# Storing six rows of one image over four DMA engines instead of sixteen, in a convolution kernel

## The chip, the cores and the metric

The kernel runs on one core of a Trainium2 chip. The metric is the device time of one execution in microseconds (us). All comparisons are between runs made on the same chip in the same rounds.

The core has 16 DMA engines, which carry everything between memory and the core's buffers. TensorE does the matmuls (PE, its weight loads PEld), VectorE is DVE, ScalarE ACT, GpSimd POOL, and SP issues transfers.

## The reference

A 3x3 convolution with padding 1. There are 16 images of 64 channels, 64 x 64 points each, and 128 output channels, all in float32:

```python
x = randn(16, 64, 64, 64);  weight = randn(128, 64, 3, 3) * 0.1
output[b, co] += weight[co, ci, kh, kw] * x_pad[b, ci, kh:kh+64, kw:kw+64]   # summed over ci, kh, kw
```

The output is 33.5 MB and the input 16.8 MB, so the DMA engines have some 50 MB to carry.

## The kernel before

Images are worked on in eight pairs. A pair's input lies on 128 partitions (2 images x 64 channels), and its output on 128 partitions too (the 128 output channels), with both images side by side in a tile of 2 x 64 x 64 numbers per partition. All transfers are issued by SP. The loads of the first seven pairs are issued at the start; from then on a pair's store is issued when its last DVE addition is done.

```python
for p in range(NP):                       # 8 pairs
    for blk in range(4):                  # 8 row pairs each
        U  = group([(G1, None)])          # matmuls
        ... us = ACT copies of U ...
        A  = group([(G21, 1), (G0, -1)])
        for b2 in range(2):
            nc.vector.tensor_add(ots[p][:, b2, j0:j0+RB, 0, :], A[b2], us[b2])
        Bt = group([(G01, 0), (G2, 2)])
        for b2 in range(2):
            nc.vector.tensor_add(ots[p][:, b2, j0:j0+RB, 1, :], Bt[b2], us[b2])
        parts = {3: (0, 64)} if p < NP - 1 else {1: (0, 32), 3: (32, 64)}
        if blk in parts:                  # the last pair is stored in two halves
            lo, hi = parts[blk]
            keep(nc.sync.dma_start(out_pairs[p, :, :, lo:hi, :], ...[:, :, lo:hi, :]))
            if p == 2: load(LATE)
# ... = cut
```

## Time and profile before

| | before |
|---|---|
| median of the runs | 127.7 us |
| span of the profiled execution | 126.6 us |
| PE busy | 84% |
| last DVE addition ends | 112.8 us |
| last store issued / landed | 112.84 / 125.6 us |
| main DMA queue | 50.63 MB, 95.1% of 16 engines' span |

### The profile page before, as it was taken

How to read it: one execution, taken by the hardware profiler on the slowest of the kernel's cores; microseconds unless marked ns; L12 is line 12 of the kernel's file. 1: busy time of each engine (PE TensorE's matmuls, PEld its weight loads, DVE VectorE, ACT ScalarE, POOL GpSimd, SP SyncE). 2: the span in 40 equal slices, each digit the busy share in tenths (PEclk: the TensorE clock that was granted, in tenths of full speed). 3: DMA queues.
4: the chain of work that ended last, by engine and by line, in shares of the span. 5: the costliest groups of instructions: out<-in, count | busy, mean ns of one | idle time of the engine just before them, and what ended most of it. 6: DMA issues, size and time to landing. Idle time of an engine off the chain costs nothing.

```text
span 126.6 us, 2424 instructions
## 1 busy us (share of the span) xinstructions
PE 106.0 (84%) x978; PEld 55.8 (44%) x978; DVE 84.3 (67%) x135; ACT 65.5 (52%) x98; POOL 33.3 (26%) x22
## 2 busy tenths in 40 slices
PE   0489999999999999999999999999999999920000
PEld 0334555555555555555555555555555555500000
DVE  0287777777777777777877787778777877760000
ACT  4283999998789876666333333336666333300000
POOL 2000395930780075007600660068000000000000
PEclk9999999999999999999999999999999999999555
DMA  4999999999999999999999999999999999999940
GB/s 116 322 422 435 424 430 419 450 419 424 430 440 437 409 442 409 435 435 419 440 414 435 424 419 435 430 435 430 414 430 445 424 424 419 432 417 424 432 184 13
DMA packets 4186, 50.77 MB, mean 401 GB/s; under 512 B 336, under 2 KB 336, under 8 KB 976
## 3 DMA queue, kind: packets, MB, share of 16 engines
q1 hardware_dynamic: 4176, 50.63, 95.1%
q8 instruction: 7, 0.11, 0.3%
q14 instruction: 3, 0.02, 0.0%
HBM read 17.07 MB, written 33.55 MB: 400 GB/s over the span
## 4 chain that ended last, share of the span: by engine, by line
PE 82%; DMA 4%; DVE 2%; issue 1%; DVEq 0%; SPq 0%
PE acc L174 82%; DMA xf<-in_x_dram 4%; DVE ot L194 1%; DVE ss L98 1%; DVEq L230 0%; DVE ot L197 0%; SPq L48 0%; DVEq L194 0%
## 5 line engine op out<-in xcount | busy, mean ns | idle before, releaser
L174 PE MATMUL acc<-xs,Wt 64*128 64x504 f16 (+3 forms) x768 | 88.9, 378 | 0.0
L174 PEld LDWEIGHTS <-Wt 64*128 64x128 f16 x960 | 54.7, 95 | 50.9 <-issue 3.3
L194 DVE TENSOR_TENSOR ot<-acc,ut 128x512 f32<-128x512 f32 x64 | 41.2, 686 | 21.9 <-PE acc L174 18.2
L188 ACT COPY ut<-acc 128x512 f32<-128x512 f32 x64 | 34.4, 590 | 39.7 <-issue 35.2
L197 DVE TENSOR_TENSOR ot<-acc,ut 128x512 f32<-128x512 f32 x64 | 41.1, 683 | 0.2 <-PE acc L174 0.2
L75 ACT CAST xs<-xf 128x1024 f16<-128x1024 f32 (+2 forms) x30 | 30.9, 1065 | 0.7 <-DMA xf<-in_x_dram 0.7
L174 PE MATMUL acc<-ss,Wt 64*128 64x504 f16 (+1 forms) x192 | 27.1, 384 | 1.2 <-DVE ss L98 1.2
L98 POOL TENSOR_TENSOR ss<-xs 128x1024 f16<-128x1024 f16 x8 | 16.8, 2124 | 30.8 <-PE acc L174 30.8
L98 POOL TENSOR_TENSOR ss<-xf 128x1024 f16<-128x1024 f32 x6 | 14.1, 2363 | 23.5 <-DMA xf<-in_x_dram 14.9
L116 PE MATMUL wp<-ident,w 128*64 128x128 f16 x18 | 1.3, 329 | 4.2 <-DVE w L88 4.2
L98 DVE TENSOR_TENSOR ss<-xf 128x512 f16<-128x512 f32 x4 | 2.8, 689 | 2.8 <-DMA xf<-in_x_dram 2.8
L116 PEld LDWEIGHTS <-w 128*64 128x64 f16 x18 | 1.1, 211 | 4.2 <-DVE w L88 4.2
L88 DVE CAST w<-w_raw 128x576 f16<-128x576 f32 x1 | 0.5, 460 | 3.7 <-DMA w_raw<-in_weight_dram 3.7
L118 ACT CAST Wt<-wp 128x384 f16<-128x384 f32 x1 | 0.5, 479 | 2.9 <-PE wp L116 2.9
L75 POOL CAST xs<-xf 128x896 f16<-128x896 f32 x2 | 1.9, 926 | 0.0
L118 ACT ACT_TABLE_LOAD x1 | 1.3, 1283 | 0.7 <-PEq L219 0.7
L123 ACT CAST Wt<-wp 128x384 f16<-128x384 f32 x1 | 0.5, 479 | 0.5 <-DVE Wt L121 0.5
L120 DVE TENSOR_TENSOR Wt<-wp,Wt 128x384 f16<-128x384 f32 x1 | 0.6, 550 | 0.0
L121 DVE TENSOR_TENSOR Wt<-wp,Wt 128x384 f16<-128x384 f32 x1 | 0.5, 547 | 0.0
L124 ACT CAST Wt<-wp 128x384 f16<-128x384 f32 x1 | 0.5, 485 | 0.0
masks.py:199 POOL TENSOR_SCALAR_AFFINE_SELECT ident<-ident 128x128 f16<-128x128 f16 x1 | 0.3, 295 | 0.1
masks.py:197 POOL MEMSET ident<- 128x128 f16 x1 | 0.2, 205 | 0.3 <-POOLq L219 0.3
(4 smaller groups left out, 0.4 us busy)
## 6 DMA issues: line engine op xcount, KB each, us to landing
out_dram<-ot SPq DMA_DIRECT2D x7, 4096.0 KB, 21.1
xf<-in_x_dram SPq DMA_DIRECT2D x7, 2048.0 KB, 21.2
out_dram<-ot SPq DMA_DIRECT2D x2, 2048.0 KB, 13.6
xf<-in_x_dram SPq DMA_DIRECT2D x2, 512.0 KB, 6.1
xf<-in_x_dram SPq DMA_DIRECT2D x1, 576.0 KB, 4.9
xf<-in_x_dram SPq DMA_DIRECT2D x1, 448.0 KB, 7.2
w_raw<-in_weight_dram SPq DMA_DIRECT2D x1, 288.0 KB, 3.0
```

Of the source, the lines that this page charges most:

```text
L75: keep(copy(xs[p][:, lo:hi, :], xf[p][:, lo:hi, :]))
L88: keep(nc.vector.tensor_copy(w16, w_raw))
L98: eng.tensor_add(ss[p][:, lo : lo + n, :], v[:, lo : lo + n, 0, :], v[:, lo : lo + n, 1, :])
L116: nc.tensor.matmul(wp[q : q + 64, k * CO : k * CO + CO], w16[:, t::9], ident)
L118: keep(nc.scalar.copy(wrow(G1), wps[1]))
L120: keep(nc.vector.tensor_sub(wrow(G21), wps[2], wrow(G1)))
L121: keep(nc.vector.tensor_sub(wrow(G01), wps[0], wrow(G1)))
L123: keep(nc.scalar.copy(wrow(G0), wps[0]))
L174: nc.tensor.matmul(tiles[b2][:, lo - j0 : hi - j0, c_lo:c_hi], Wt[p0 : p0 + 64, wi, kw, :], rhs, start=i == 0, stop=i == n - 1,)
L188: keep(nc.scalar.copy(ut, U[b2]))
L194: nc.vector.tensor_add(ots[p][:, b2, j0 : j0 + RB, 0, :], A[b2], us[b2])
L197: nc.vector.tensor_add(ots[p][:, b2, j0 : j0 + RB, 1, :], Bt[b2], us[b2])
```

## The change

Its intent is to move a little of the DMA work from most of the engines to four of them. Pair 5's store (the sixth pair) is cut in four. Six rows of its second image go by two transfers that cover 124 and 4 partitions, and neither number can be divided evenly over 16 engines.

```diff
-                keep(nc.sync.dma_start(
-                    out_pairs[p, :, :, lo:hi, :],
-                    ots[p].rearrange("p b j i c -> p b (j i) c")[:, :, lo:hi, :],
-                ))
+                src = ots[p].rearrange("p b j i c -> p b (j i) c")
+                dst = out_pairs[p]
+                if p == 5:
+                    keep(nc.sync.dma_start(dst[:, 0, :, :], src[:, 0, :, :]))
+                    keep(nc.sync.dma_start(dst[:, 1, 0:58, :], src[:, 1, 0:58, :]))
+                    for q0, q1 in ((0, 124), (124, 128)):
+                        keep(nc.sync.dma_start(dst[q0:q1, 1, 58:64, :], src[q0:q1, 1, 58:64, :]))
+                else:
+                    keep(nc.sync.dma_start(dst[:, :, lo:hi, :], src[:, :, lo:hi, :]))
```

## The prediction

> **What bounds the kernel now.** I read the page's slices first, then its chain that ended last, then the DMA queue's own waits, and last a table of stretches over the end of the run.
>
> In the slices PE and DMA both look full. They are the rows of busy tenths and of moved data, 40 slices of 3.17 us:
>
> ```profile
> PE   0489999999999999999999999999999999920000
> DMA  4999999999999999999999999999999999999940
> GB/s 116 322 422 435 424 430 419 450 419 424 430 440 437 409 442 409 435 435 419 440 414 435 424 419 435 430 435 430 414 430 445 424 424 419 432 417 424 432 184 13
> ```
>
> PE is empty in the last four to five slices while DMA goes on at full rate for most of them. The chain of waits names PE, but it follows compute instructions only and stops where the last one stops:
>
> ```profile
> PE acc L174 82%; DMA xf<-in_x_dram 4%; DVE ot L194 1%; DVE ss L98 1%; DVEq L230 0%; DVE ot L197 0%; SPq L48 0%; DVEq L194 0%
> ```
>
> In order of time its last piece is the DVE addition at 112.22 us, 0.60 us long, so it ends at 112.8. The span is 126.6. The 13.8 us after it belong to the stores. The queue's own waits say the same; L230 is the end of the program:
>
> ```profile
> SPq L230 <- DMA out_dram<-ot: 12.4, 2, 7.5
> ```
>
> The table of stretches shows how that tail runs out. Its columns are the busy times of PE, PEld, DVE, ACT and POOL, the granted clock, the mean share of the 16 DMA engines that is busy, and GB/s:
>
> ```profile
> 100.00:110.00 10.00, 10.00 (x96) 5.26 (x94) 7.57 (x13) 3.58 (x7) 0.00 (x0) 1.00 1.00 424
> ...
> 118.00:120.00 2.00, 0.00 (x0) 0.00 (x0) 0.00 (x0) 0.00 (x0) 0.00 (x0) 0.50 1.03 438
> 120.00:121.00 1.00, 0.00 (x0) 0.00 (x0) 0.00 (x0) 0.00 (x0) 0.00 (x0) 0.50 0.87 369
> 121.00:122.00 1.00, 0.00 (x0) 0.00 (x0) 0.00 (x0) 0.00 (x0) 0.00 (x0) 0.50 0.54 229
> 122.00:123.00 1.00, 0.00 (x0) 0.00 (x0) 0.00 (x0) 0.00 (x0) 0.00 (x0) 0.50 0.24 98
> 123.00:124.00 1.00, 0.00 (x0) 0.00 (x0) 0.00 (x0) 0.00 (x0) 0.00 (x0) 0.50 0.08 33
> 124.00:125.00 1.00, 0.00 (x0) 0.00 (x0) 0.00 (x0) 0.00 (x0) 0.00 (x0) 0.50 0.06 25
> ```
>
> Until 120 us all 16 engines are busy and the rate stays at 424 to 438 GB/s, so the kernel is bound by what the DMA engines carry: 50.63 MB on this queue, 3.164 MB an engine. Then they drop out one after another. A share of 0.06 is one engine of 16, and 25 GB/s is one engine's rate (424/16 = 26.5). So **the end is set by the one engine that is last**, alone for its last 2 us. A transfer over 16 engines gives each the same bytes, but they don't work at the same pace.
>
> To see why, I took the trace's individual transfer records. They don't name their engine, so I joined them into 16 sequences, each record starting where another ended; this is inference. Five sequences finish at about 120.7 to 120.9, two at 121.3 to 121.4, seven at 122.1 to 122.4, one at 123.13 and one at 125.17. The cluster of seven and some others each met one 16 KB instruction fetch (7 of them, 0.88 to 1.01 us each, each on another engine). The last one has no such fetch: from 41 to 111 us, but for a pause about 70 to 77, its 16 KB packets take some 645 ns where the others take 611. So one engine is slow by itself.
>
> **What the Trainium skill says.** "DMA: Bandwidth & Descriptors", section "Why a DMA increments its semaphore by 16 and not by 1": the engines used are the largest k up to 16 that divides the slowest dimension's size on both sides, and on the hardware queues the lowest-numbered k are used. For 124 and for 4 that gives 4, so engines 0 to 3. This trace has only transfers of 128 partitions, with 16 semaphore increments for each of its 21, which agrees as far as it goes; k = 4 is not shown yet. The same page, section "Latency and other measured facts", says that engines 7 and 15 are usually slower in traces and guesses at a cause tied to software queues. The trace agrees that one engine is slow (645 against 611 ns), on a hardware queue; it doesn't show which. "Runtime: NRT & Kernel Launch", section "Instruction fetch mechanics", says that instructions are refilled in 16 KiB blocks by DMA; the seven 16,384-byte packets of the instruction queue agree.
>
> **The change part by part.** Pair 5's 4 MB store, issued at 87.23 us, becomes four: image 0 whole, 58 rows of image 1, and the last six rows of image 1 in two pieces of 124 and 4 partitions. The bytes are the same.
>
> *Issue.* Three more issues on SP at 0.37 us (the issue's duration): 1.1 us on a queue that otherwise waits 36.7 us for DVE between 80 us and the end. At 87.2 the engines still hold most of pair 4's store (issued at 74.42, landing between 91.8 and 95.5), so none runs dry. Cost: 0.
>
> *Semaphores.* The landings use 8 semaphores in turn, so a later transfer takes one again. With three more, pair 6 and the two halves of pair 7 take those of transfers landed by 85 us. Cost: 0. No compute instruction waits for pair 5's store, as its slot is not used again. Cost: 0.
>
> *Bytes moved.* Six rows are 6 x 64 x 4 = 1,536 B a partition, 196,608 B in all. Over 16 engines that is 12,288 B each; over four it is 49,152 B. So engines 4 to 15 lose 12,288 B, and 0 to 3 gain 36,864 B.
>
> *Time of it.* From the records, back to back, a 16,384 B packet takes 608 ns, 8,192 B 306, 4,096 B 153, 2,304 B 90. That is nearly straight, 0.037 ns a byte and a few ns fixed. A 14,848 B packet is then about 551 ns and a 1,536 B one about 62 (estimates). Engines 4 to 15: 8 x (551 - 608) = -456 ns, and one more semaphore write of 9 ns: **-0.45 us** (about -0.47 at the slow engine's pace). Engines 0 to 3: the same -0.45, plus 31 + 1 = 32 packets of 62 ns = +1.98, plus two semaphore writes: **+1.55 us**.
>
> *Sum.* If the slow engine is one of 4 to 15, it ends at 125.17 - 0.45 = 124.7. The latest that one of engines 0 to 3 could have ended is 123.13; with 1.55 it comes to 124.7 as well, no later. If they are of the usual 120.7 to 122.4, they come to 122.3 to 124.0. So the end moves by about -0.45 us: 127.7 - 0.45 = 127.25. It can't be more: the transfers take no more off it.
>
> **The rivals.**
> 1. *The slow engine is among 0 to 3.* Then it ends at 125.17 + 1.55 = 126.7, and the time is about 129.3 (+1.2%). For: nothing in the trace tells its number; by chance alone 4 of 16. Against: the skill's note on 7 and 15, and that a change so oddly shaped looks made to relieve the others. I give it 15%.
> 2. *Small packets cost more than the line says*, or four engines reading rows of the low partitions' store in 1.5 KB pieces slow each other. With double the cost, 124 ns, engines 0 to 3 gain 3.5 us and end at 124.2 to 125.9, or later if the 123.13 one is among them; the time would be 127 to 129. For: writes to memory in pieces of 1.5 KB occur nowhere in this trace (the small packets are loads, and the first ones of the run took up to 0.9 us). Against: 2,304 B packets ran at 90 ns once the queue was going. 10%.
> 3. *The slow engine's slowness is the profiler's.* The profiled execution took 128.41 us against a median of 127.7 without it. If the slow engine ends 0.7 us earlier unprofiled, it still ends after 123.13, so the gain is kept unless the 123.13 one is among 0 to 3; then the time would be about 127.9. 10%.
> 4. *PE or DVE is the bound* and the transfer is hidden anyway. Against: they end at 112.8, and the last store isn't free to go before 112.84 but is queued behind stores that land at 115.9 and 120.7. Nothing for it.
>
> **Range and chances.** The middle case gives 127.25. Repeats of the kernel before spread over 0.27 us (127.53 to 127.8), and a partly lost gain is more likely than a larger one, so I say 127.3. The range 126.9 to 128.1 holds the middle case with noise and the partly lost gains, and leaves out most of rival 1. Faster by over 2% needs -2.55 us, more than five times what is taken off the last engine: 1%. Slower by over 2% needs +2.55 us: rival 1 with rival 2 together, 3%.
>
> **What would show it.** In the profile after: 24 transfers; small packets rise by 128 under 2 KB. The last addition is still at about 112.8. If right, in the stretches of the tail the share at 121 to 123 us is higher than 0.54 and 0.24, because four engines run 1.55 us longer, and the single engine's tail ends near 124.7 in place of 125.2. The table after 123.5 tells the rivals apart: four engines (share 0.25) running past 124 means rival 2, one engine running to about 126.7 means rival 1. The prediction is wrong if the pieces spread over all 16 engines (then no change beyond noise, 127.7), if the slow engine is another in each execution, or if it is one of the lowest four.

## The result, and the profile after

The changed kernel took 126.99 us (median of 6 runs, 126.78 to 127.37) against 127.69 us of the kernel before in the same rounds (6 runs, 127.4 to 127.8). The ratio is 0.9952, with a 95% interval of 0.9934 to 0.997. A ratio here is the mean time of one kernel's fast runs over that of the other's of the same rounds, so it is not quite the ratio of the medians. The gain is real and small, 0.4 to 0.8 us.

The page of the kernel after, the packet count and the main queue:

```profile
DMA packets 4338, 50.77 MB, mean 405 GB/s; under 512 B 360, under 2 KB 488, under 8 KB 1128
...
q1 hardware_dynamic: 4328, 50.63, 96.2%
```

The bytes are the same 50.63 MB. Packets under 512 B are the semaphore writes: 360 against 336 before. The arithmetic is 336 - 16 (the one store) + 16 + 16 + 4 + 4 = 360, so both odd pieces ran on four engines. The difference between 488 and 360 is the 128 packets of 1,536 B.

The SP's wait at the end of the program, kernel after (us in total, times, longest):

```profile
SPq L236 <- DMA out_dram<-ot: 9.5, 2, 4.8
```

It was 12.4 before. Part of the difference is not the change's: in this execution the compute ran later. The last piece of the chain that ended last, kernel after (start, length):

```profile
113.69 0.60 DVE ot L197
```

So the last addition ended at 114.3 us, 1.5 us later than before. That lateness was there before the changed code was reached: pair 3's store was issued at 63.09 us against 61.62. **Compute came 1.5 us later, and the span was still 1.3 us shorter (125.3 against 126.6).** This pair of traces alone shows that compute doesn't set the end.

The stretches of the tail, kernel after, with the columns of the prediction's table (busy times, clock, share of the 16 engines, GB/s):

```profile
120.00:121.00 1.00, 0.00 (x0) 0.00 (x0) 0.00 (x0) 0.00 (x0) 0.00 (x0) 0.50 0.97 410
121.00:122.00 1.00, 0.00 (x0) 0.00 (x0) 0.00 (x0) 0.00 (x0) 0.00 (x0) 0.50 1.01 426
122.00:123.00 1.00, 0.00 (x0) 0.00 (x0) 0.00 (x0) 0.00 (x0) 0.00 (x0) 0.50 0.26 107
123.00:124.00 1.00, 0.00 (x0) 0.00 (x0) 0.00 (x0) 0.00 (x0) 0.00 (x0) 0.50 0.10 41
124.00:125.30 1.30, 0.00 (x0) 0.00 (x0) 0.00 (x0) 0.00 (x0) 0.00 (x0) 0.50 0.00 0
```

The engines now stop closer together: 1.01 at 121 to 122 us, where it was 0.54, and the engine that ran alone to 125 us is gone from the last row. Two caveats. First, the full row at 121 to 122 is in part the later compute: some engines had run dry and were behind for that reason. The rows around the issue of pair 6's store (101.51 us), kernel after:

```profile
100.00:102.00 2.00, 2.00 (x22) 1.04 (x20) 1.48 (x3) 1.07 (x2) 0.00 (x0) 1.00 0.80 331
102.00:104.00 2.00, 2.00 (x22) 1.01 (x20) 1.94 (x4) 0.00 (x1) 0.00 (x0) 1.00 1.04 436
```

A share counts packets by their start; 0.80 means that there was less to start than 16 engines could take. Before, it was 0.99 in the first of these. The same sequences of packets that I used for the prediction (joined by time, as the records don't name their engine) show idle time of up to 1.7 us there, on engines that are not last in the end. The slow engine has none: its next packet follows its last write for pair 5 at once, at 104.0 us.

Second, the end moved by more in this trace than the change can move it: the last landing is at 124.5 us against 125.6. The slow engine can be followed to see why. From about 40 us on, four packets in each 2.5 us take clearly longer than the rest (some 644 ns for 16 KB against 611, and in the trace after 578 to 601 for the 14,848 B packets against 554), which is the rate of a single engine. Each engine ends its share of a transfer with a 4-byte semaphore write, and a write that lies directly beside these slow packets is the slow engine's. Its writes, in us (the last column is from unrounded times):

| run | end of pair 4's store | end of pair 5's store | pair 5's share took |
|---|---|---|---|
| before | 95.00 | 105.28 | 10.28 |
| edit at pair 6 (pair 5's store whole) | 94.44 | 104.72 | 10.29 |
| cut without the move | 94.69 | 105.05 | 10.36 |
| after | 94.16 | 104.00 | 9.84 |
| after, repeated | 94.53 | 104.37 | 9.84 |
| twelve rows | 94.00 | 103.36 | 9.36 |

So the change takes 0.44 us off the slow engine's share and twelve rows take 0.92; the sums said 0.45 and 0.9. **The slow engine's pace in these stores is the same in each execution followed** (in nine traces its share of an untouched 4 MB store takes 10.28 to 10.33 us), **but how late it comes to the changed store is not**: in this trace it was 0.84 us ahead of the kernel before already at the end of pair 4's store, which the change doesn't touch. So the size of the gain is read from the rounds, not from one pair of traces.

The same marks show when this engine is slow. Its slow packets begin at about 41 us in both traces, when the stores start to move. In the trace after there are none from 69.4 to 74.2 us, while it carries its share of the late load of pair 7. They end at 111.7 us before and at 113.0 after, though the stores go on to 125.2 and 124.0; TensorE's last matmul ended at 111.5 and 112.9. So the engine was slow in stores made while the compute engines ran, and not in that load or in the stores after the compute. What slows it is not shown.

### The profile page after: what moved, and what is told of

Read it like the earlier page. It is cut to its first block, busy times and chain, and to the rows that moved or that the text cites. A ratio compares the mean times of both kernels' runs of the same rounds, so it can differ in the third digit from the quotient of the medians.

```text
span 125.3 us, 2428 instructions
## 1 busy us (share of the span) xinstructions
PE 106.9 (85%) x978; PEld 54.6 (44%) x978; DVE 84.3 (67%) x135; ACT 65.5 (52%) x98; POOL 33.4 (27%) x22
## 3 DMA queue, kind: packets, MB, share of 16 engines
q1 hardware_dynamic: 4328, 50.63, 96.2%
## 4 chain that ended last, share of the span: by engine, by line
PE 83%; DMA 4%; DVE 2%; issue 1%; DVEq 0%; SPq 0%
PE acc L174 83%; DMA xf<-in_x_dram 4%; DVE ot L194 1%; DVE ss L98 1%; DVE ot L197 0%; DVEq L236 0%; SPq L48 0%; DVEq L194 0%
## 5 line engine op out<-in xcount | busy, mean ns | idle before, releaser
L174 PEld LDWEIGHTS <-Wt 64*128 64x128 f16 x960 | 53.4, 96 | 53.8 <-issue 5.1
```

Of the source, the lines that this page charges most:

```text
L174: nc.tensor.matmul(tiles[b2][:, lo - j0 : hi - j0, c_lo:c_hi], Wt[p0 : p0 + 64, wi, kw, :], rhs, start=i == 0, stop=i == n - 1,)
```

## The experiments

The theory: the end is set by one DMA engine that works at a slower pace than the rest for most of the run and is never idle; the change is worth what it takes off that engine. The rivals: the gain comes from cutting the 4 MB store into smaller ones; or place and time of the transfers matter, not the bytes per engine. All outputs were correct in all runs.

### The cut without the move

```diff
-                    for q0, q1 in ((0, 124), (124, 128)):
-                        keep(nc.sync.dma_start(dst[q0:q1, 1, 58:64, :], src[q0:q1, 1, 58:64, :]))
+                    keep(nc.sync.dma_start(dst[0:128, 1, 58:64, :], src[0:128, 1, 58:64, :]))
```

> Pair 5 cut as in the change (image 0, 58 rows, 6 rows), but the six rows go by one transfer of 128 partitions over all 16 engines. Moving-bytes theory (the gain is the 12,288 B taken off the engines that end last): every engine carries what it did before, so no gain: ratio to before 0.998 to 1.002, about 127.7 us. Rival (the gain comes from cutting the 4 MB store into smaller ones): as the change, ratio about 0.995, about 127.1 us.

Measured: ratio 1.001 (0.998 to 1.0041), 127.96 against 127.81 us. The cut by itself brings nothing; even the interval's low end is above the middle of the changed kernel's. The tail of this run:

```profile
122.00:123.00 1.00, 0.00 (x0) 0.00 (x0) 0.00 (x0) 0.00 (x0) 0.00 (x0) 0.50 0.29 123
123.00:124.00 1.00, 0.00 (x0) 0.00 (x0) 0.00 (x0) 0.00 (x0) 0.00 (x0) 0.50 0.06 25
124.00:125.00 1.00, 0.00 (x0) 0.00 (x0) 0.00 (x0) 0.00 (x0) 0.00 (x0) 0.50 0.06 25
```

It is the tail of the kernel before again: one engine, 25 GB/s, alone for 2 us.

### Twice the dose

Twelve rows in place of six by 124 and 4 partitions (52 rows over all engines):

```diff
-                    keep(nc.sync.dma_start(dst[:, 1, 0:58, :], src[:, 1, 0:58, :]))
+                    keep(nc.sync.dma_start(dst[:, 1, 0:52, :], src[:, 1, 0:52, :]))
                     for q0, q1 in ((0, 124), (124, 128)):
-                        keep(nc.sync.dma_start(dst[q0:q1, 1, 58:64, :], src[q0:q1, 1, 58:64, :]))
+                        keep(nc.sync.dma_start(dst[q0:q1, 1, 52:64, :], src[q0:q1, 1, 52:64, :]))
```

> As the change with twelve rows in place of six: engines 4 to 15 carry 24,576 B less than before (-0.9 us), engines 0 to 3 carry 73,728 B more (+3.1 us). Moving-bytes theory: engines 0 to 3 become the last, ending near 120.7 to 122.4 plus 3.1, so the gain is gone: 127.5 to 128.6 us. Rival (only the relief of the slow engine counts, engines 0 to 3 have slack to spare): twice the gain, about 126.5 us.

Measured: ratio 1.0022 (0.9992 to 1.0051), 128.04 us. The gain is gone, as the theory has it. The sequences of this trace that hold the small packets, so engines 0 to 3, end at 123.4, 123.7, 124.3 and 124.8 us; the slow one ends at 123.4. Its tail, where several engines now run out together (0.21 is three to four of 16):

```profile
123.00:124.00 1.00, 0.00 (x0) 0.00 (x0) 0.00 (x0) 0.00 (x0) 0.00 (x0) 0.50 0.21 90
124.00:125.00 1.00, 0.00 (x0) 0.00 (x0) 0.00 (x0) 0.00 (x0) 0.00 (x0) 0.50 0.04 16
```

What is taken off each of twelve engines is put on each of the other four at three times the amount, so there is a best dose. Of none, six and twelve rows, six is the best; where the best lies between them was not tested.

### Is it engine 15?

32 rows by pieces of 120 and 8 partitions, so that 15 and 8 engines take them:

```diff
-                    ... 58 rows, then 6 rows by (0, 124), (124, 128)
+                    for q0, q1, r0, r1 in ((0, 128, 0, 32), (0, 120, 32, 64), (120, 128, 32, 64)):
+                        keep(nc.sync.dma_start(dst[q0:q1, 1, r0:r1, :], src[q0:q1, 1, r0:r1, :]))
```

> 32 rows of image 1 by transfers of 120 and 8 partitions, which should take 15 and 8 engines: engine 15 carries 65,536 B less (-2.45 us), engines 0 to 7 carry 8,192 B more (+0.3 us), 8 to 14 the same. If the slow engine is engine 15: the end falls to the next engines, ratio 0.980 to 0.988, about 125.2 to 126.2 us. If the slow engine is one of 4 to 14: ratio 0.999 to 1.003, 127.6 to 128.1 us.

Measured: ratio 1.0054 (1.0013 to 1.0094), 128.47 us. It is not engine 15, whose relief by 65 KB changed nothing for the better. I had set 0.999 to 1.003 for the other case and forgot a part of it: if the slow engine is one of 0 to 7, it takes the 8-partition piece too, +0.3 us or +0.24%, which the interval holds. The landings say that it is so. These are the times (us) at which the engines of the 8-partition piece reported, from the trace's semaphore records:

```
101.7 101.9 102.0 102.0 102.6 102.7 102.7 106.4
```

Eight engines, and one of them comes 3.7 us late: **the slow engine is one of 0 to 7.** The same records of the kernel after give 102.9, 103.0, 103.6 and 103.7 for the 124-partition piece and 104.5 for the last arrival of the 58-row piece before it. That late engine is not one of 0 to 3.

### Marks of different sizes

Image 1 of pair 5 stored in five pairs of pieces, each with a row count of its own:

```diff
+   (0,128, rows 0:14), (0,126 / 126,128, 14:28), (0,108 / 108,128, 28:40),
+   (0,120 / 120,128, 40:50), (0,119 / 119,128, 50:58), (0,124 / 124,128, 58:64)
```

> A look only. Pair 5's image 1 is stored in pieces of 126+2, 108+20, 120+8, 119+9 and 124+4 partitions with a row count of its own for each, so that packet sizes mark which engines are among the lowest 14, 2, 12, 10, 15, 8, 7, 9 and 4. Theory that the slow engine is 15 or 7: the sequence of packets that is slow (about 645 ns for 16 KB) has no packets of the 120-partition piece (15), or has the 8-partition piece's packet and no 119-partition packets (7). Rival: any other of 4 to 14. No claim on the time, which engines 0 to 3 may set (some 2.9 us more than before on 0 and 1).

Measured: 131.75 us, one look. The marking worked less well than hoped, because joining the small packets into sequences by time failed. Also, with 12 stores in a row SP ran into its own earlier transfers' semaphores; it was busy with the pieces to 104.2 us, pair 6's store was issued at 104.39 us, and the late compute hides the tail. The landings could be read: the 8-partition piece has late arrivals at 105.6 and 106.0, while the nine arrivals of the 9-partition piece are the seven of the 119-partition piece plus 0.1 to 0.2 us, and two more at 103.1 and 103.2, which must be engines 7 and 8. So engine 7 is not late, and the late one is in 0 to 6; with the last section, in 4 to 6.

### Five engines, and six

Twelve rows by 125 + 3 partitions (5 and 3 engines), and by 114 + 6 + 6 + 2 (6, 6, 6 and 2):

```diff
-   (0,128, rows 0:58), (0,124 / 124,128, rows 58:64)
+   (0,128, rows 0:52), (0,125 / 125,128, rows 52:64)                          # five
+   (0,128, rows 0:52), (0,114 / 114,120 / 120,126 / 126,128, rows 52:64)      # six
```

> Twelve rows by transfers of 125 and 3 partitions (5 and 3 engines). Landings of the runs so far put the slow engine among 4 to 6. Engines 5 to 15 carry 24,576 B less (-0.9 us), engines 0 to 4 some 54 KB more (+2.0 us; 0 to 2 a few packets more). If the slow engine is 5 or 6: it ends 0.9 us sooner, others of 0 to 4 at 122.9 to 124.5, ratio 0.992 to 0.998. If it is engine 4: it ends 2 us later, ratio about 1.015.

> Twelve rows by transfers of 114, 6, 6 and 2 partitions (6, 6, 6 and 2 engines). Engines 6 to 15 carry 24,576 B less (-0.9 us), engines 0 to 5 some 41 KB more (+1.6 us). If the slow engine is 6 (or, against the landings, 7 or above): ratio 0.990 to 0.996. If it is 4 or 5: ratio about 1.012.

Measured: five engines, ratio 1.0158 (1.0139 to 1.0178), +2.0 us; six, 1.0141 (1.0122 to 1.016), +1.8 us. They were run on another chip. One run of the first (172.84 us, clock 0.67) is left out. The first lands on the branch written for engine 4, the second on that for engine 4 or 5. The sum for engine 4 in the first: 25 packets of 3,072 B at 118 ns (their 121 ns less the 3 ns by which packets overlap) are +2.95 us, less 0.9 for the shorter rows, +2.05. In the second: 21 packets, +2.48, less 0.9, +1.6. For engines 5 and up the first would have been a relief of 0.9 us. The slow engine's own semaphore writes agree: with six engines its share of pair 5's store took 11.95 us (94.26 to 106.21) against 10.28, so +1.67. The tail with six engines:

```profile
123.00:124.00 1.00, 0.00 (x0) 0.00 (x0) 0.00 (x0) 0.00 (x0) 0.00 (x0) 0.50 0.12 49
124.00:125.00 1.00, 0.00 (x0) 0.00 (x0) 0.00 (x0) 0.00 (x0) 0.00 (x0) 0.50 0.06 25
125.00:126.00 1.00, 0.00 (x0) 0.00 (x0) 0.00 (x0) 0.00 (x0) 0.00 (x0) 0.50 0.06 25
```

The lone engine's end has moved out by a full row. Its landings show where the late engine sits: pieces of 114, of 6 and again of 6 partitions (six engines), then of 2 (two engines):

```
114: 102.9 103.0 103.3 103.8 104.0 106.5
6:   103.1 103.1 103.5 104.0 104.2 106.7
6:   103.3 103.3 103.7 104.2 104.3 106.9
2:   103.9 104.5
```

The late arrival is in each of the six-engine pieces and not in the two-engine one.

The five-engine kernel, one more look:

> The twelve rows over five engines again, for a trace in the fast state (the first profile fell in a slow one). If the slow engine is engine 4, the landing of the 125-partition piece (5 engines) has one late arrival some 2 us or more after the others, and the last landing of the run is about 2 us later than in the kernel before, alone for its last 2 to 4 us; time near 129.7 us. If it is another, no late arrival in that piece.

Measured: 129.34 us. It was run on another chip. The 125-partition piece landed at 103.4, 103.5, 104.2, 106.0 and 107.0, and the 3-partition piece at 103.6, 103.7 and 104.4. So the two late ones are engines 3 and 4, neither of 0 to 2. That is one more late arrival than I expected, and this run alone doesn't tell which of the two is engine 4. The slow packets of 16 KB (647 and 644 ns) go on directly after the later write, so the slow engine is the one that came at 107.0: its share of pair 5's store took 12.41 us, 2.13 more than before. The run's last landings were at 126.2 and 126.7, so no engine ran alone for 2 us, and the end is 1.1 us after that of the kernel before (125.6), not 2; that part of the expectation failed, as the slow engine was 0.95 us ahead already at the end of pair 4's store (94.05 against 95.00). The arrival at 107.0 fits the theory: less the 2.95 us of its 25 packets it is 104.0, and the last arrival of the 52-row piece was 103.9.

### The yardstick, and another place

The changed kernel again, and the same edit at pair 6 (`if p == 6:`):

> The changed kernel again, as the yardstick of this chip. Moving-bytes theory: ratio 0.994 to 0.998, as on record (0.9952).

> The same edit made to the seventh pair's store (issued near 100 us) in place of the sixth's. Theory: the last engine is never idle, so it matters only what it carries, not when: ratio as the changed kernel's, 0.994 to 0.998. Rival: the extra bytes of engines 0 to 3 were hidden in the idle time that the trace of the changed kernel shows before the seventh pair's store; placed after it they are not, and the gain is less: ratio 0.998 to 1.003.

Measured: the changed kernel 0.9979 (0.9951 to 1.0006), 127.24 against 127.61 us; with the edit at pair 6, 0.9962 (0.994 to 0.9984), 127.16 us. The rival held that the extra bytes of engines 0 to 3 were paid for by idle time before pair 6's store. Placed after that time they should then have cost something; they did not. In the two places tried it is what the engine carries that counts, not when. The repeat's interval just touches 1. The forecast of -0.45 us (0.9965) lies in all three intervals, the one on record and these two; the chip's noise does not allow a closer size.

### An attempt at a better version

If engine 4 alone is slow, one would like to relieve it without loading 0 to 3 threefold. Pieces issued from GpSimd, meant to fall on engines 0 to 4 and 5 to 15 (that they do isn't shown):

```diff
                     keep(nc.sync.dma_start(dst[:, 0, :, :], src[:, 0, :, :]))
+                    for q0, q1 in ((121, 126), (0, 121), (126, 128)):
+                        keep(nc.gpsimd.dma_start(dst[q0:q1, 1, 30:58, :], src[q0:q1, 1, 30:58, :]))
-                    keep(nc.sync.dma_start(dst[:, 1, 0:58, :], src[:, 1, 0:58, :]))
+                    keep(nc.sync.dma_start(dst[:, 1, 0:30, :], src[:, 1, 0:30, :]))
                     ... (0, 124), (124, 128) for rows 58:64, as in the change
```

> An attempt at a better version: the six rows as in the change, and 28 further rows of the same image issued from GpSimd in pieces of 5, 121 and 2 partitions, which should take engines 0 to 4, then 5 to 15, then 2 more. Engine 4 would carry some 50 KB less there and 12 KB less by the six rows (-2.3 us), engines 5 to 15 some 9 KB more net, so the end would fall to about 122.8: ratio 0.980 to 0.988. Rival: the software path spreads 121 partitions over all 16 engines, 8 each, and relieves only engine 15: ratio as the changed kernel's or above, 0.995 to 1.005. Second rival: issuing from GpSimd costs more than it brings.

Measured: ratio 1.0105 (1.0061 to 1.0149), 129.59 us: slower. It was run on another chip. The page of this run, its queues:

```profile
q1 hardware_dynamic: 4328, 49.71, 93.4%
q0 software_dynamic: 208, 0.92, 2.1%
```

On the main queue 1% of the span per 0.532 MB (49.71/93.4), on this one per 0.438 MB (0.92/2.1): its bytes cost more engine time. Its 7,168 B packets took 331 ns in the mean with a median of 272, and a part of the main queue's packets slowed beside them (7,680 B: mean 365, median 291). Whether engine 4 was relieved can't be read from this trace, since each of these transfers reports 16 arrivals whatever engines it uses. The attempt failed, and which of its two rivals is the cause stays open.

## Why the prediction was right

**What bounds the kernel.** Right. The end is set by a DMA engine that is never idle, not by PE. The trace after has its last addition 1.5 us later and its end 1.3 us earlier.

**How many engines.** Right: 360 semaphore writes, and four arrivals for each of the two odd pieces.

**The terms of the sum.** The 1,536 B packets took 65 ns and the 14,848 B ones 554; less 3 ns of overlap that is 62 and 551, as estimated. Engines 0 to 3, forecast to end at 122.3 to 124.0, ended at 122.1, 122.3, 122.9 and 123.6. The slow engine was to lose 0.45 us (0.47 at its own pace) and lost 0.44 of its share. It was forecast to end at 124.7 (its last packet) and came at 124.0, but that difference is not the change's: it was 0.84 us ahead before the first changed transfer.

**The step that was left to chance**, that the slow engine is not one of 0 to 3, held. The experiments narrow it to engine 4, the first one that the change relieves. On chip 15 they do so alone: twelve rows over five engines cost 2 us, so it is one of 0 to 4, and in the repeat of the change its packets pass from the 58 rows straight to pair 6's store, without one of the odd pieces, so it is none of 0 to 3. That was luck on my side; I had leaned on 7 and 15, and it is neither.

**A step that failed.** "So none runs dry" was worked out at the issue of pair 5's store and holds there, but some engines ran dry 14 us later, before pair 6's. It cost nothing, because they were not the last ones. "The last addition is still at about 112.8" failed as well, by a lateness that began before the change. The prediction's "one engine is slow by itself" says too much: the pause that the prediction saw about 70 to 77 us is the load of pair 7, and the slowness ends with the compute. The sum didn't need it.

**The rivals.** The slow engine among 0 to 3: no. Small packets at double cost: no, 65 ns. That the slowness is the profiler's: not tested, every run of these rounds comes with its span and granted clock. That it lasts only while the engines compute leaves this rival open. PE or DVE as the bound: no.

**The size.** Forecast -0.45 us, measured -0.6 us by the ratio (0.0048 x 127.7), interval -0.4 to -0.8; -0.3 in the repeat and -0.5 at pair 6. The forecast can't be told from these. The trace's own reading of the step is -0.44.

Left open: why engine 4 is slow, and only in stores while the engines compute. It was so on more than one chip, with the same 10.28 to 10.33 us: on chip 15 it is engine 4; on chip 9 the landings leave 0 to 6 and the twelve-row trace leaves 4 and up (the slow packets pass straight from the 52 rows to pair 6's store); on chip 5, 3 or 4.

## What to carry to other kernels

When DMA is the bound, look at how the transfers run out, engine by engine: a mean of 95% can hide one engine that works 2 us longer than all the others. A partition count that divides badly is a tool to shift work between engines, here only from the upper ones to the lowest few, and with four of them what comes off each of the others lands threefold on each of the four; so dose it and test the dose on both sides. To find what one engine does, look for what marks its records: here a slow packet and the semaphore write beside it gave its share of one store to 0.01 us, where the whole time is known to some 0.2 us. Test a cut and a move separately, as the cut alone brought nothing here.

## What the Trainium skill lacked or had wrong

- "DMA: Bandwidth & Descriptors", section "Latency and other measured facts", names engines 7 and 15 as the usually slow ones and suggests a cause that belongs to software queues. Here the slow engine was engine 4 (on chip 15; the runs on chips 9 and 5 agree as far as they go), by the page's own numbering of the lowest k: 645 ns for a 16 KB packet against 611, on a hardware queue. Relief of engine 15 by 65 KB gained nothing (1.0054), and loading a fifth engine cost 2.0 us (1.0158).
- The same page, section "Why a DMA increments its semaphore by 16 and not by 1", has the rule for k and was right in all cases tried: 124, 4, 120, 8, 126, 2, 108, 20, 119, 9, 125, 3, 114 and 6 partitions gave 4, 4, 15, 8, 14, 2, 12, 10, 7, 9, 5, 3, 6 and 6 arrivals. It doesn't say that k below 16 can be used to balance engines (0.9952 with six rows, 1.0022 with twelve).
- No page says that an engine can be slow in one kind of transfer and at one time only. Here it took 10.28 to 10.33 us for its share of a 4 MB store while the engines computed (16 packets, some 644 ns each), the same in each execution followed, and 4.82 us for its eight packets of pair 7's load in the trace after (15.13 for that load and the next store, less 10.31, an estimate).
